# Where the preparation steps of a later block are written in a loop over sixteen experts: from the ninth expert on, five each, instead of from the second on, two each

## The chip, the cores and the metric

The kernel runs on one core of a Trainium2 chip. The metric is the device time of one execution in microseconds (us), as a median of several runs. One more execution was profiled; its span goes from the first to the last instruction.

The core has five engines that run side by side, each with its own queue of instructions in a fixed order: TensorE (PE; its weight loads stand as PEld), VectorE (DVE), ScalarE (ACT), GpSimd (POOL) and SyncE (SP), which here only sends off loads. They wait for each other by semaphores. Transfers between HBM and the on-chip memory run on 16 DMA engines.

## The reference, cut to what matters

The reference runs two blocks of two layers each, one after the other, on 256 tokens of width 1024. The second layer of the first block ends in a routed mixture of 16 experts ("the second experts" of this kernel). The second block begins with a layer that has a state-space part (S5).

```python
def expert_block(args):                      # routed_moe, for each expert
    xblk, e = args
    hid = jax.nn.silu(xblk @ w_gate[e]) * (xblk @ w_up[e])
    return hid @ w_down[e]
...
def s5_ssm(u, a_re, a_im, log_dt, b_re, b_im, c_re, c_im, d_skip, glu_w, glu_b):
    lam = lax.complex(a_re, a_im)
    dt = jnp.exp(log_dt)[:, None]
    lam_bar = jnp.exp(lam * dt)
    b_bar = ((lam_bar - 1.0) / lam)[..., None] * b_mat
    bu = jnp.einsum('bsgh,gph->bsgp', ug, b_bar)
    _, states = lax.associative_scan(combine, (a_seq, bu), axis=1)
    y = jnp.real(jnp.einsum('bsgp,ghp->bsgh', states, c_mat))
```

The scan of the state-space part needs things that depend on its weights alone: dt, the powers of lam_bar, b_bar and a layout of C. They don't need the experts' results, so the kernel computes them beside the experts.

## The kernel before, in words

The second experts are `run_small`. For each expert e of 0 to 15 it needs 12 MB of weights, in twelve loads of 1 MB (`wload`, L172): four for gate, four for up, four for down. All loads go through SP's queue, in the order up(e), gate(e+1), down(e), up(e+1). Their buffers are a ring of 14 (`NW`, pool `W`); other stages and tables take buffers of the same ring. The ring is full when the loop starts.

Per expert TensorE computes the gate product G and the up product U (L1303, 32 matmuls each), four transposes of the hidden rows (L1348, into the PSUM buffer "tp", of which there is one here), and the down product Y (L1303, 32 matmuls). Beside them it gathers the rows of the expert after next (`rows`, xp L1475 and rs L1481; xp uses "tp" as well) and adds the finished expert to its token rows (acc, L1507). ScalarE applies silu to G (L1317). VectorE multiplies by U (s, L1328), copies the transposed hidden rows (hTe, L1349), scales the gathered rows (L1485 to L1487) and weights Y (L1498). As written, the order within an expert is: rows(e+1), up(e), the acc of e-1, **the side steps**, gate(e+1) with the hidden transposes of e in its middle, down(e).

The side steps are those of the generator `ssm_prep`, called by `side_step` (L1558). `side_step` ties the instructions of a step behind the current expert's s on VectorE, and behind an earlier instruction on GpSimd; on the other engines nothing ties them. The Tile scheduler lays down the final order of each engine, and hands out the buffers of a pool.

`ssm_prep` yields 22 times, so it has 22 steps with work:

- Step 1 sends loads of a_re, a_im and log_dt from GpSimd, turns them by three transposes through "tp" (L1929) and computes dt on VectorE by a polynomial. Step 2 computes sines, cosines and the exponential on VectorE (L1853 to L1942), step 3 the factors of b_bar (L1948 to L1963).
- Step 4 loads b_re and b_im, forms b_bar (L1980 to L1982) and transposes it in two groups of four through "tp" (L1986), copied to LB by ScalarE.
- Step 5 loads c_re and c_im (L1994), spreads them on VectorE (L1996), and transposes them in two groups through "tp" (L1999). The load buffers are three of a tag, "wl", so that c_im has to wait for the one that step 4 uses to the end.
- Step 6 claims four buffers of the ring of 14 for the rotation tables rotE (`unit`, whose first write of 0.5 KB goes through SP's queue, L153), clears their starts on GpSimd, and doubles the tables' filled length for the first time. Steps 7 to 10 double it again, from 2 to 32 columns; from 32 columns on, each of the four tables has a step of its own (steps 11 to 22). A doubling of one table is four instructions of VectorE (L2025, L2027, L2028, L2030) and two of GpSimd (L2026, L2029).

Before, steps are called two at a time in experts 1 to 14, so that the last one runs at expert 11. The rest of the calls find nothing left.

Of the kernel before, what the change touches and what calls it, by code (L numbers as in the profile page):

```python
# [22 lines left out]
NE = 16  # L23
# [63 lines left out]
class Kern:  # L87
# [1375 lines left out]
    def run_small(self, NT, wg, wu, wd, R, add_ps, over, after, side=None):  # L1463


        nc, w, ps, CB = self.nc, self.wk, self.ps, 64
        ld = lambda W: (lambda k: self.pre.pop(0) if self.pre else self.wload(W, k, 2, 0, D))
        acc = [[ps.tile([P, 512], F32, name="acc", tag="acc", bufs=2 * NT) for _ in range(2)] for _ in range(NT)]

        def rows(e):  # L1470
            tp = ps.tile([P, 8, CB], F32, name="xp", tag="tp", bufs=self.tpb)
            for k in range(8):
                for i in range(3):
                    for t in range(NT):
                        nc.tensor.matmul(tp[:, k, :], self.hb[:, t, i, k * P:(k + 1) * P], R["oh"][:, t, e],  # L1475
                                         start=(i == 0 and t == 0), stop=(i == 2 and t == NT - 1))
            xT = w.tile([P, 8, CB], F32, name="xT", tag="xT", bufs=2)
            rs = ps.tile([P, CB], F32, name="rs", tag="G", bufs=1)
            for i in range(3):
                for t in range(NT):  # L1480
                    nc.tensor.matmul(rs, self.rb3[:, t, i], R["oh"][:, t, e], start=(i == 0 and t == 0), stop=(i == 2 and t == NT - 1))  # L1481
            rc = w.tile([P, CB], F32, name="rc", tag="rc", bufs=1)
            nc.scalar.copy(rc, rs)
            gain, shift = (v[:, :, None].to_broadcast([P, 8, CB]) for v in self.gs2)
            nc.vector.tensor_tensor(xT, tp, rc[:, None, :].to_broadcast([P, 8, CB]), op=OP.mult)  # L1485
            nc.vector.tensor_tensor(xT, xT, gain, op=OP.mult)
            self.last_v = nc.vector.tensor_tensor(xT, xT, shift, op=OP.add).ins  # L1487
            return xT

        def sums(e, Y):  # L1490
            ohT = w.tile([P, NT, P], F32R, name="ohT", tag="ohT", bufs=1)
            for t in range(NT):
                nc.vector.tensor_scalar(ohT[:, t], self.K["iota"], tokt[:, t, e:e + 1], None, op0=OP.is_equal)
            yh = w.tile([P, 512], F32R, name="yh", tag="yh", bufs=1)
            yl = w.tile([P, 512], F32R, name="yl", tag="yl", bufs=1)
            wr = R["wrow"][:, e:e + 1]
            yt = w.tile([P, 512], F32, name="yt", tag="yt", bufs=1)
            nc.vector.scalar_tensor_tensor(yt, Y, wr, self.g2, op0=OP.mult, op1=OP.mult)  # L1498
            nc.scalar.copy(yh, yt)
            nc.vector.tensor_tensor(yl, yt, yh.bitcast(F32), op=OP.subtract)  # L1500

            def f():
                for c in range(2):
                    for t in range(NT):
                        r = slice(64 * c, 64 * c + 64)
                        for y in (yh, yl):
                            nc.tensor.matmul(acc[t][c], ohT[r, t], y[r], start=(e == 0 and y is yh), stop=(e == NE - 1 and y is yl))  # L1507
            return f

        def ahead(k):  # L1510

            if k < 2:
                return ld(wd[0])(k)
            v = [self.hl.tile([P, 1024], F32, name="wa", tag=tag) for tag in ("wh", "wl")]
            for i in range(2):
                nc.sync.dma_start(v[i], wd[0][(k + i) * P:(k + i + 1) * P, :])
            return v

        xT = rows(0)
        first = self.last_v  # L1520
        s = self.gate(CB, xT, ld(wg[0]))
        with self.tc.issue_after(first):
            R.pop("rest")()
        tokt = w.tile([P, NT, NE], F32, name="tokt", tag="tokt", bufs=1)
        for t in range(NT):
            nc.vector.tensor_scalar(tokt[:, t], R["tokf"], -float(P * t), None, op0=OP.add)
        pend = None
        for e in range(NE):
            if side and e == NE - 1:
                while self.side_step(side):  # L1530
                    pass
            xn = rows(e + 1) if e + 1 < NE else None
            self.up(CB, s, xT, ld(wu[e]))
            if e == NE // 2:
                self.late = [self.last_v, self.last_s, self.last_m, self.last_dma]
            if pend:
                pend()
            for _ in range(2):
                if side and 0 < e < NE - 1:
                    self.side_step(side)  # L1540
            hT = []
            old = s
            turn = lambda: hT.append(self.hidden_T(CB, old))
            if e + 1 < NE:
                s = self.gate(CB, xn, ld(wg[e + 1]), turn)
            else:
                turn()
            xT = xn
            pend = sums(e, self.down(CB, None, ld(wd[e]) if e else ahead, None, None, hT[0]))
        self.gains2()  # L1550
        pend()
        for c in range(2):
            for t in range(NT):
                add_ps(t, c, acc[t][c], c)
        over()
        after()
# [887 lines left out]
```

## Time and profile before

| | us |
|---|---|
| median of 3 runs | 2193.2 (2193.14 to 2193.75) |
| profiled execution, its time | 2193.03 |
| profiled execution, its span | 2191.5 |
| PE busy in the span | 1984.8 (91%) |
| VectorE busy | 1397.7 (64%) |
| ScalarE busy | 954.7 (44%) |
| GpSimd busy | 305.3 (14%) |

Busy shares are means over stages that differ. The second experts run from 1,284 us (first gate product) to 1,758 us (last sum), so what bears on the change is read from this stretch.

### The profile page before, as it was taken

To read this page: it belongs to the slowest core of one execution; us is meant where nothing else is said; L and a number is where in the kernel's file an instruction comes from. 1 tells how busy PE (TensorE), PEld (TensorE's weight loads), DVE (VectorE), ACT (ScalarE), POOL (GpSimd) and SP (SyncE) were. 2 spreads that over 40 slices of the span, in tenths; PEclk is the share of its full clock that TensorE was granted. 3 is DMA by queue.
4 is the path that set the end of the run, shared out by engine and by line. 5 is a ranking of instruction groups with operands and counts; after the bars stand their busy time and mean duration, and the time that the engine had idled before them with its cause. 6 is when DMAs were issued, how large, how long until landed. Compare 5 with 4: busy or idle time off the path is not lost. (4 is left out here: it accounts for less than half of the span.)

```text
span 2191.5 us, 30093 instructions
## 1 busy us (share of the span) xinstructions
PE 1984.8 (91%) x11482; PEld 1357.3 (62%) x11483; DVE 1397.7 (64%) x2526; ACT 954.7 (44%) x1435; POOL 305.3 (14%) x370
## 2 busy tenths in 40 slices
PE   6999979969999999998979979899888889898998
PEld 2877654647778888776675533333333266776997
DVE  3457666669999999888757644332331179576767
ACT  2435315437778787776545610000000032555443
POOL 1201122140000000011020010110100025231111
PEclk9999989979999999999999989999999999989999
DMA  8544367749999999999332579999999954425460
GB/s 251 135 145 136 135 239 273 289 164 351 366 369 389 379 389 388 378 348 332 140 117 58 214 304 353 389 408 409 408 409 409 406 172 143 137 97 181 158 209 20
DMA packets 191307, 580.52 MB, mean 265 GB/s; under 512 B 18736, under 2 KB 49904, under 8 KB 186032
## 3 DMA queue, kind: packets, MB, share of 16 engines
q1 hardware_dynamic: 176656, 550.03, 67.7%
q0 software_dynamic: 7760, 23.26, 3.6%
q10 hardware_dynamic: 6736, 5.21, 0.8%
q8 instruction: 93, 1.52, 0.3%
q14 instruction: 62, 0.51, 0.1%
HBM read 568.41 MB, written 10.03 MB: 264 GB/s over the span
## 5 line engine op out<-in xcount | busy, mean ns | idle before, releaser
L189 DVE TENSOR_TENSOR wl<-wch,wh 128x1024 fp32r<-128x1024 f32 x518 | 631.5, 1239 | 146.3 <-ACT wh L188 129.7
L188 ACT CAST wh<-wch 128x1024 fp32r<-128x1024 f32 x524 | 545.6, 1053 | 292.0 <-PE pj L210 63.6
L211 PE MATMUL pj<-h,wl 128*128 128x256 f32 x448 | 131.0, 293 | 6.3 <-DVE wl L189 6.3
L209 PE MATMUL pj<-h,wh 128*128 128x256 f32 x448 | 130.9, 294 | 3.3 <-ACT h L487 1.3
L210 PE MATMUL pj<-h,wh 128*128 128x256 f32 x448 | 130.4, 292 | 0.0
L1317 ACT ACTIVATE s<-G 128x512 f32<-128x512 f32 x16 | 9.6, 597 | 274.1 <-PE G L1303 274.1
L1303 PE MATMUL G<-wch,xT 128*64 128x512 f32 x512 | 126.5, 621 | 1.2 <-DMA wch<-in_moe_w_gate_dram 1.2
L1303 PE MATMUL U<-wch,xT 128*64 128x512 f32 x512 | 119.8, 599 | 3.7 <-DMA wch<-in_moe_w_up_dram 3.2
L1303 PE MATMUL Y<-wch,hTe 128*64 128x512 f32 x488 | 110.5, 597 | 6.8 <-DMA wch<-in_moe_w_down_dram 5.3
L210 PE MATMUL G<-wl,xu 128*128 128x512 f32 x256 | 103.0, 402 | 5.0 <-DVE wl L189 4.8
L210 PE MATMUL U<-wl,xu 128*128 128x512 f32 x256 | 102.8, 402 | 3.3 <-DVE wl L189 2.3
L209 PE MATMUL U<-wh,xu 128*128 128x512 f32 x256 | 101.5, 397 | 3.2 <-ACT wh L188 3.2
L210 PE MATMUL Y<-wl,hu 128*128 128x512 f32 x256 | 102.8, 402 | 1.4 <-DVE wl L189 1.2
L209 PE MATMUL Y<-wh,hu 128*128 128x512 f32 x256 | 100.7, 393 | 2.6 <-ACT wh L188 2.4
L209 PE MATMUL G<-wh,xu 128*128 128x512 f32 x256 | 101.3, 396 | 0.0
L211 PE MATMUL U<-wh,xu 128*128 128x512 f32 x256 | 100.5, 393 | 0.0
L211 PE MATMUL Y<-wh,hu 128*128 128x512 f32 x256 | 100.5, 393 | 0.0
L211 PE MATMUL G<-wh,xu 128*128 128x512 f32 x256 | 100.1, 391 | 0.0
L211 PEld LDWEIGHTS pj<-h,wl 128*128 128x128 f32 x448 | 88.4, 198 | 9.6 <-DVE wl L189 7.1
L209 PEld LDWEIGHTS pj<-h,wh 128*128 128x128 f32 x448 | 88.5, 198 | 6.9 <-ACT wh L188 2.5
L210 PEld LDWEIGHTS pj<-h,wh 128*128 128x128 f32 x448 | 88.7, 198 | 1.9 <-issue 1.7
L209 PE MATMUL mm<-wh,hTh 128*128 128x256 f32 (+1 forms) x256 | 81.1, 318 | 3.5 <-DVE Y L693 1.8
(667 smaller groups left out, 4185.3 us busy)
## 6 DMA issues: line engine op xcount, KB each, us to landing
wch<-in_moe_w_gate_dram SPq DMA_DIRECT2D x128, 1024.0 KB, 8.0
wch<-in_moe_w_up_dram SPq DMA_DIRECT2D x128, 1024.0 KB, 9.0
wch<-in_moe_w_down_dram SPq DMA_DIRECT2D x125, 1024.0 KB, 8.3
wch<-in_ada_w_dram SPq DMA_DIRECT2D x40, 1024.0 KB, 6.6
wch<-in_even_w_in_dram SPq DMA_DIRECT2D x34, 1024.0 KB, 5.6
wch<-in_odd_w_in_dram SPq DMA_DIRECT2D x16, 1024.0 KB, 5.5
wch<-in_even_w_out_dram SPq DMA_DIRECT2D x10, 1024.0 KB, 5.0
wch<-in_ada_w_dram SPq DMA_DIRECT2D x32, 256.0 KB, 6.6
```

Of the source, the lines that this page charges most:

```text
L188: self.last_h = nc.scalar.copy(h, v).ins
L189: self.last_l = e.tensor_tensor(l, v, h.bitcast(F32), op=OP.subtract).ins
L209: m(out, lh, rh, start=first, stop=False, skip_group_check=chk)
L210: m(out, lh, rl, start=False, stop=False, skip_group_check=chk)
L211: self.last_m = m(out, ll, rh, start=False, stop=last, skip_group_check=chk).ins
L1303: self.last_m = nc.tensor.matmul(out[f * 64:f * 64 + 64, :], x[:, k, :], v[k - k0][:, f * 512:(f + 1) * 512], start=(k == 0), stop=(k == 7 ...
L1317: self.last_s = nc.scalar.activation(s, G, AF.Silu).ins
```

## The change

The loop that calls the side steps calls five instead of two, and from expert 8 (the ninth) instead of expert 1. The 22 steps so fall on experts 8, 9, 10, 11 (five each) and 12 (two). Nothing that is computed changes.

```diff
@@ -1535,8 +1535,10 @@
             if pend:
                 pend()
-            for _ in range(2):
-                if side and 0 < e < NE - 1:
+
+
+            for _ in range(5):
+                if side and NE // 2 <= e < NE - 1:
                     self.side_step(side)
             hT = []
             old = s
```

## Rows read from the trace of the kernel before

**Rows 1.** The page, part 2: GB/s moved, in 40 equal slices.
```profile
GB/s 251 135 145 136 135 239 273 289 164 351 366 369 389 379 389 388 378 348 332 140 117 58 214 304 353 389 408 409 408 409 409 406 172 143 137 97 181 158 209 20
```

**Rows 2.** Stretches from U to U: length, busy us by engine, PEclk, DMA, GB/s.
```profile
1343.70:1377.10 33.40, 29.68 (x174) 10.80 (x172) 11.99 (x36) 2.60 (x5) 1.66 (x10) 0.95 0.91 344
...
1467.45:1495.20 27.75, 26.01 (x166) 9.55 (x164) 7.32 (x17) 1.43 (x3) 1.99 (x4) 1.00 1.02 408
...
1583.10:1615.20 32.10, 27.61 (x166) 10.18 (x164) 11.79 (x17) 1.43 (x3) 2.87 (x2) 0.95 1.02 408
...
1674.60:1705.30 30.70, 26.75 (x164) 9.02 (x164) 5.37 (x10) 1.43 (x3) 0.00 (x0) 1.00 1.02 409
```

**Rows 3.** The same view, in stretches of 30 us.
```profile
1350.00:1380.00 30.00, 26.22 (x157) 9.70 (x155) 11.51 (x34) 2.60 (x5) 1.66 (x10) 0.94 0.90 336
...
1380.00:1410.00 30.00, 26.64 (x165) 10.02 (x163) 7.38 (x27) 2.49 (x5) 2.20 (x13) 0.94 1.00 380
```

**Rows 4.** SP's timeline: start, us, line, operation, output<-input, count.
```profile
1342.23 7.15 SPq L172 DMA_DIRECT2D wch<-in_moe_w_up_dram  x4
...
1351.31 13.11 SPq L153 DMA_DIRECT2D rotE<-in_const_dram  x4
...
1366.55 7.67 SPq L172 DMA_DIRECT2D wch<-in_moe_w_gate_dram  x4
```

**Rows 5.** PE's timeline, expert 2; in brackets idle time before, its releaser.
```profile
1352.82 1.89 PE L1303 MATMUL G<-wch,xT 128*64 128x512 f32 x8
...
1358.34 0.89 PE L1986 MATMUL tp<-c_ident,pr 128*128 128x128 f32 x4 [3.64 <-DVE pr L1982]
...
1359.17 3.31 PE L1303 MATMUL G<-wch,xT 128*64 128x512 f32 x6
...
1364.00 0.66 PE L1348 MATMUL tp<-c_ident,s 128*128 128x128 f32 x4
```

**Rows 6.** PE's timeline, experts 6, 10 and 13.
```profile
1477.54 0.66 PE L1348 MATMUL tp<-c_ident,s 128*128 128x128 f32 x4 [0.79 <-DVE s L1328]
...
1488.26 7.09 PE L1303 MATMUL Y<-wch,hTe 128*64 128x512 f32 x32
...
1600.29 1.60 PE L1475 MATMUL xp<-ohb,hb 128*128 128x64 bf16 x36 [2.86 <-DVE hTe L1349]
...
1674.57 1.94 PE L1303 MATMUL U<-wch,xT 128*64 128x512 f32 x8 [0.61 <-DMA wch<-in_moe_w_up_dram]
```

**Rows 7.** Stretches of side steps on VectorE (columns as in rows 2).
```profile
1326.41:1339.92 13.51, 13.51 (x115) 5.55 (x113) 12.73 (x82) 0.81 (x2) 0.00 (x0) 1.00 1.03 409
...
1353.64:1360.76 7.12, 3.48 (x14) 1.19 (x11) 6.70 (x28) 0.59 (x1) 0.00 (x0) 0.85 1.03 408
...
1419.24:1423.14 3.90, 2.56 (x14) 1.03 (x15) 3.90 (x34) 0.00 (x0) 2.84 (x14) 1.00 1.03 412
...
1448.06:1453.44 5.38, 4.24 (x20) 1.57 (x21) 5.28 (x32) 0.00 (x0) 3.60 (x13) 1.00 1.02 404
...
1505.13:1507.60 2.47, 2.33 (x12) 0.90 (x12) 2.47 (x9) 0.00 (x0) 1.23 (x2) 1.00 1.04 415
...
1562.74:1567.11 4.37, 2.52 (x12) 1.00 (x13) 4.37 (x9) 0.00 (x0) 2.33 (x2) 1.00 1.02 409
...
1593.06:1599.56 6.50, 4.24 (x20) 1.57 (x21) 6.50 (x9) 0.00 (x0) 2.87 (x2) 1.00 1.02 409
...
1625.14:1629.95 4.81, 4.24 (x20) 1.57 (x21) 4.81 (x9) 0.00 (x0) 0.00 (x0) 1.00 1.02 409
```

**Rows 8.** POOL's second C load; landing times of both C loads.
```profile
1361.05 0.75 POOL L1994 DMA_DIRECT2D pr<-in_ssm_c_im_dram  x1 [42.92 <-DVE pr L1982]
...
DMA to landing us min/median/max: 5.1/6.7/8.2
```

**Rows 9.** VectorE's timeline: a hidden copy, a product s.
```profile
1364.70 0.69 DVE L1349 COPY hTe<-tp 128x512 f32<-128x512 f32 x1 [3.94 <-PE tp L1348]
...
1476.80 0.69 DVE L1328 TENSOR_TENSOR s<-s,U 128x512 f32<-128x512 f32 x1 [3.11 <-PE U L1303]
```

## The prediction

> **What bounds the kernel now.** I read the page's 40 slices first [rows 1]: in slices 27 to 32 (1,424 to 1,753 us) the second experts load at 406 to 409 GB/s and nothing else in the kernel stays at that rate so long, so the change lies in a stretch near its load limit. Next, the stretches from one expert's up product U to the next one's [rows 2]. Numbered from 0, expert 6 takes 27.75 us, expert 10 takes 32.10 and expert 13 takes 30.70. Expert 13 is paced by loads: its U begins when its load lands, at 1,674.57 [rows 6]. Twelve loads of 1 MB in 30.7 us are 2.56 us a load. Expert 6 never waits for a load: 27.7 us is TensorE's own pace, so **TensorE has 3.0 us of slack per expert**. It starts with a full ring of 14 loaded buffers and has used this lead up only by expert 13, because the side steps stop it on the way.
>
> Loads therefore set the end: the last experts wait for them, and a load lost anywhere is lost for good. Where are they lost? In 30 us windows [rows 3]: 336 GB/s at 1,350 to 1,380 and 380 at 1,380 to 1,410, against 409 when full [rows 2]. (73 + 29) GB/s x 30 us are 3.06 MB, or **7.5 us at 409 GB/s**. The load queue shows why [rows 4]: after the up loads at 1,342 the four rotE writes hold it from 1,351.31 to 1,364.42, because each waits for a weight buffer to come free, and the next gate load goes out at 1,366.55. So early, most of the ring of 14 holds data that TensorE has not reached, and few loads are under way to bridge such a pause.
>
> **What the change does, part by part.** The 22 steps that do work (five of preparation, 17 of the rotation tables) run at experts 8 to 12 (5, 5, 5, 5, 2) instead of 1 to 11 (2 each). No instruction is added or removed.
>
> **1. The ring of weight buffers.** The rotE buffers are claimed after the up loads of expert 9, not of expert 3. TensorE's pace brings it to U of expert 8 at 1,343.7 + 6 x 27.7 = 1,509.9 [rows 2]. The loads allow it at 1,674.57 - 5 x 30.7 - 7.5 = 1,513.6 [rows 2, 3, 6]. So TensorE will by then wait for loads, nearly all free buffers are queued loads (up to 12, or 31 us), and four small writes no longer drain that queue. The pause of rows 4 goes: **-7.5 us** (between 0, if as much is lost at the new place, and -7.5).
>
> **2. The first batch, at expert 8.** Each preparation step that transposes takes the one PSUM buffer "tp". So do the transposes of the hidden rows (L1348) that the down product needs. Rows 5 show that they get it in the order written: at expert 2 the product s was ready, yet L1348 ran at 1,364.00, behind the transposes of L1986 (first at 1,358.34, for which TensorE had stood 3.64 us). With five steps ahead of it, L1348 of expert 8 queues behind the whole preparation. Its length: steps 1 and 2 take 13.5 us on VectorE [rows 7], of which some 2.7 are four copies and products of the experts at 0.69 [rows 9]; steps 3 and 4 take 7.1; together 17.9. Then the second C load goes out only when step 4 has released its buffer (POOL stood until L1982, 1,361.05) and lands 5.1 to 8.2 us later, median 6.7 [rows 8]. Until now an expert's work lay between; in one batch VectorE waits for it, with the hidden copy queued behind. The product s, the C product, transposes, copies and hand-overs are about seven pieces of 0.6 to 0.7 us [rows 5, 9], 4.5. Sum: 17.9 + 6.7 + 4.5 = 29.1 us from s to the down product (27.5 to 30.6). Without side steps that way is 1,488.26 - 1,476.80, or 11.5 us (L1348 follows s by 0.74) [rows 6, 9]. The down product is **17.6 us late** (16 to 19). What hides some of it is only the gate product of 7 us, and that is in the 11.5. After the idle time the clock is down: six matmuls took 3.31 us after the 3.64 us stop, where eight take 1.89 at full clock [rows 5], so +1.9. Together 19.5 (16 to 22). The loads a_re to the first C load don't move: POOL has no other work here and sends them as soon as their buffers are free.
>
> **3. The later batches, experts 9 to 12.** The hidden copy stands behind the table steps on VectorE. Before, two such steps took from 2 to 6.5 us [rows 7], where six of nine such stretches stand, and TensorE waited 2.86 us for the copy at the longest [rows 6]: 6.5 less 3.65 that 16 gate matmuls cover. With all 32 the cover is 7.3 (1.85 for each eight more [rows 5]). Now: expert 9 some 2 (the first, smallest tables; not shown, taken as half of the next) + 3.9 + 5.4 = 11.3, less 7.3, plus 1.9 of low clock: 5.9. Expert 10: 2 x 2.47 + half of 4.37 = 7.1, less 3.65: 3.5. Expert 11: 1.5 x 4.37 + 6.5 = 13.1, less 7.3, plus 1.9: 7.7. Expert 12: 4.81 - 3.65 = 1.2. **Sum 18** (8 if the copy slips in between steps that wait for POOL; 25 if the cover stays at 16 matmuls).
>
> Two equal batches in rows 7 took 6.50 us with POOL busy for 2.87 us beside them and 4.81 with POOL idle, so POOL's share of a table step slows VectorE's. The Trainium skill (GPSIMD Engine Reference, section 1, Specifications) says that GpSimd's SBUF interfaces are shared with VectorE and contend with VectorE instructions of two SBUF inputs. That agrees with the two rows, and it speaks against packing five such steps together.
>
> **The sum.** From U of expert 8 to U of expert 15 there are seven stretches with 3.0 us slack, 21 us, plus 2.0 for one gather of rows fewer (expert 15 is the last) and 0.8 because the last down product need not wait for loads: 23.8. Late at the end: 19.5 + 18 - 23.8 = 13.7 us behind loads that themselves come 7.5 us earlier: **+6.2 us**. Everything after the experts begins when they end, so it moves along. The profiled execution took 2,193.03 us (span 2,191.5), 0.17 below the median of the runs: 2193.03 + 6.2 = 2,199.2, and on the median some **2,199 us**.
>
> **The rivals.**
> (a) Faster: the hidden transposes don't queue behind the preparation, or VectorE's batches fall into TensorE's waits for loads. For it: at expert 8 TensorE waits for loads anyway, and in rows 5 gate matmuls run between the side transposes. Against it: L1348 in rows 5. Then lateness stays under the 23.8 us of slack, loads set the end, and the 7.5 us are won: 2,185.7. It decides if parts 2 and 3 together cost less than 24 us rather than 37.5.
> (b) No change: the gain is eaten up just so, 31.3 us of stops: 2,193, if the C load lands in 5.1 us and the later batches cost some 13.
> (c) Much slower: POOL beside VectorE stretches all batches as in rows 7 (1.35 times), and 24 + 22 us of stops end 22 us behind the loads: 2193.2 - 7.5 + 22.2 = 2,208.
> (d) It does nothing: the scheduler keeps the order of the engines. Against it: steps are tied behind the current expert's product s. 2,193.
>
> **How the numbers follow.** Chances: the forecast, with ends from 2,195 to 2,204, 0.50; (a) 0.22; (b) 0.15; (c) 0.10; (d) 0.03. A measurement of this kernel tells 0.2% (4.4 us) from no change. Of the forecast's half some 0.12 lies below 2,197.6; of (b) all is within. Faster 0.23 (all of (a) and a rest), same 0.32, slower 0.45. The range takes in (a)'s time and most of (c): 2,186 to 2,207; its ends are the full gain with no lateness, and stops of 45 us in all.
>
> **What would show it.** The pause of rows 4 at 1,350 to 1,410 should be gone (409 GB/s there); TensorE should wait for loads by expert 7; a stop of 12 to 19 us should stand at expert 8, ended by L1999 or L1348; the last experts should run at 27.7 us without waiting for loads. If they wait for loads to the end, (a) is right. A load gap at the new place of the rotE writes would refute part 1.

## The result and the profile after

The changed kernel takes 2,207.1 us as a median of four runs (2,205.8 to 2,210.7), against 2,193.5 for the kernel before beside it (2,193.1 to 2,195.7). The ratio is 1.0054, with a 95% interval of 1.0037 to 1.0071. It is **slower**, by 8 to 16 us (0.4 to 0.7%). The forecast was slower by some 6 (2,199); the median lies 0.1 us beyond the upper end of the range. So the sign was right, and the size was rather less than half of what came (13.6).

The profiled execution took 2,210.65 us (span 2,209.1), 17.6 more than that of before. As the stage begins at slightly different times in the profiled executions, its length is counted below from the first gate product to the start of the last sum: 1,284.5 to 1,758.1 before, **473.5 us**, and 1,286.8 to 1,776.4 after, **489.5 us**. The stage thus holds 16.0 of the 17.6 us. (The profiled execution of the changed kernel is the longest of its four, 3.5 us above their median, so the stage shows somewhat more than the medians do.) This length is given for every experiment as "the stage".

First, stretches of 30 us of the kernel after, in the columns of [rows 2]:

```profile
1350.00:1380.00 30.00, 28.37 (x175) 10.31 (x176) 5.87 (x11) 1.43 (x3) 0.00 (x0) 1.00 1.03 409
1380.00:1410.00 30.00, 27.58 (x172) 9.94 (x169) 6.07 (x10) 1.43 (x3) 0.00 (x0) 1.00 1.02 409
1650.00:1680.00 30.00, 19.63 (x126) 7.24 (x122) 15.13 (x18) 1.43 (x3) 7.93 (x6) 0.83 0.76 291
```

The first two answer [rows 3]: where 336 and 380 GB/s stood there are 409 now. In the third, loads have fallen to 291 GB/s, and TensorE is busy for 19.6 us of 30: there the loads fall behind because TensorE stands and frees no buffers. Next, the stretches from U to U of experts 8 to 12:

```profile
1515.50:1566.20 50.70, 34.23 (x181) 13.06 (x181) 21.59 (x111) 4.84 (x9) 2.00 (x12) 0.80 0.95 367
1566.20:1601.00 34.80, 27.71 (x164) 10.71 (x164) 17.15 (x92) 0.87 (x3) 10.43 (x43) 0.85 0.87 331
1601.00:1635.40 34.40, 28.88 (x166) 10.88 (x164) 12.83 (x29) 1.43 (x3) 5.92 (x10) 0.90 0.95 368
1635.40:1674.70 39.30, 28.14 (x166) 10.18 (x164) 20.88 (x29) 1.43 (x3) 10.39 (x8) 0.87 0.83 327
1674.70:1703.50 28.80, 25.99 (x166) 9.55 (x164) 10.11 (x17) 1.43 (x3) 0.00 (x0) 1.00 1.01 400
```

Experts 2 to 5 of this kernel take 27.55 us each (from U of expert 2 at 1,344.6 to U of expert 6 at 1,454.8), so that the five stretches are 23.2, 7.3, 6.9, 11.8 and 1.3 us too long, some **50** in all. POOL, for whose work beside the experts only a rival of the prediction had a price of its own, is busy for 10.4 us in the second and the fourth.

How expert 8 is stopped is seen on TensorE, in the columns of [rows 5]:

```profile
1541.59 1.09 PE L1988 MATMUL tp<-c_ident,pr 128*128 128x128 f32 x4 [5.21 <-DVE pr L1984]
1544.15 1.09 PE L1988 MATMUL tp<-c_ident,pr 128*128 128x128 f32 x4 [1.47 <-DVE pr L1984]
1545.91 1.11 PE L2001 MATMUL tp<-c_ident,pr 128*128 128x128 f32 x4 [0.68 <-ACT LB L1989]
1551.17 1.09 PE L2001 MATMUL tp<-c_ident,pr 128*128 128x128 f32 x4 [4.15 <-DVE pr L1998]
1552.95 1.11 PE L1348 MATMUL tp<-c_ident,s 128*128 128x128 f32 x4 [0.69 <-ACT LCb L2006]
1554.85 9.91 PE L1303 MATMUL Y<-wch,hTe 128*64 128x512 f32 x32 [0.78 <-DVE hTe L1349]
```

The product s came at 1,525.15, on VectorE:

```profile
1525.15 0.69 DVE L1328 TENSOR_TENSOR s<-s,U 128x512 f32<-128x512 f32 x1 [3.79 <-PE U L1303]
```

The down product Y starts at 1,554.85, 29.7 us later. L1348 stands behind all four groups of preparation transposes (L1988 and L2001, which are L1986 and L1999 of before, two lines further down). Y then takes 9.91 us instead of 7.09 [rows 6]; the granted clock is 0.50, the lower of its two levels, from 1,545 to 1,560.

And how experts 9 to 12 are stopped:

```profile
1574.92 3.65 PE L1303 MATMUL G<-wch,xT 128*64 128x512 f32 x16
1585.37 0.32 PE L1475 MATMUL xp<-ohb,hb 128*128 128x64 bf16 x3 [6.79 <-DVE hTe L1349]
1585.62 3.68 PE L1303 MATMUL G<-wch,xT 128*64 128x512 f32 x8
...
1611.72 3.65 PE L1303 MATMUL G<-wch,xT 128*64 128x512 f32 x16
1619.27 2.08 PE L1475 MATMUL xp<-ohb,hb 128*128 128x64 bf16 x36 [3.90 <-DVE hTe L1349]
...
1646.06 5.37 PE L1303 MATMUL G<-wch,xT 128*64 128x512 f32 x24
1661.66 1.12 PE L1475 MATMUL xp<-ohb,hb 128*128 128x64 bf16 x18 [10.23 <-DVE hTe L1349]
...
1690.17 1.21 PE L1475 MATMUL xp<-ohb,hb 128*128 128x64 bf16 x36 [1.18 <-DVE hTe L1349]
```

Each time the gathering product xp, which writes "tp", waits for VectorE to empty it by the hidden copy hTe: 6.79, 3.90, 10.23 and 1.18 us. Ahead of xp stand 16, 16 and 24 gate matmuls at experts 9, 10 and 11. Eight gate matmuls right behind the first stop take 3.68 us; at full clock eight take 1.89 [rows 5].

### The profile page after: what moved, and what is told of

Its sections match the earlier page's. It is cut to its first block, busy times and chain, and to the rows that moved or that the text cites. A ratio compares the mean times of both kernels' runs of the same rounds, so it can differ in the third digit from the quotient of the medians.

```text
span 2209.1 us, 30098 instructions
## 1 busy us (share of the span) xinstructions
PE 1991.6 (90%) x11482; PEld 1365.9 (62%) x11483; DVE 1402.9 (64%) x2526; ACT 955.1 (43%) x1435; POOL 306.3 (14%) x370
## 3 DMA queue, kind: packets, MB, share of 16 engines
q10 hardware_dynamic: 6736, 5.21, 0.8%
q8 instruction: 93, 1.52, 0.3%
```

## The experiments

All ratios are to the kernel before on the same chip, with 95% intervals. Unless it is said otherwise, a diff is against the changed kernel.

**1. The second C load.** A buffer of another tag lets the load go out early, so that VectorE doesn't wait for it.

```diff
-                tc_ = hl("pr3", "wl")
+                tc_ = hl("pr3", ("wl", "wh")[c])
```

> The changed kernel with one edit: the buffer of the second C load comes from another tag, so that the load goes out with the first ones at about 1,318 us instead of behind step 4 of expert 8. Theory A (TensorE's stops at experts 8 to 12 set the end): VectorE's wait of 6.3 us for that load at expert 8 goes, the down product of expert 8 starts some 6 us earlier, and the whole is 5 to 7 us shorter than the changed kernel, about 2,201 us. Theory B (the loads that are missing after the new place of the four rotE writes set the end): that place and the ring are as before, so the time stays at 2,207.

Measured: 1.0071 (1.0048 to 1.0095), the stage 486.7 us. Theory A missed: the stage is 2.8 us shorter, and the runs show no gain (the changed kernel had 1.0054). B's time came; whether B's cause is at work, experiment 2 tells. VectorE's wait for the load is gone, but TensorE's timeline shows what was behind it:

```profile
1540.26 1.08 PE L1988 MATMUL tp<-c_ident,pr 128*128 128x128 f32 x4 [5.77 <-DVE pr L1984]
...
1544.58 1.12 PE L2001 MATMUL tp<-c_ident,pr 128*128 128x128 f32 x4 [0.68 <-ACT LB L1989]
1546.88 1.12 PE L2001 MATMUL tp<-c_ident,pr 128*128 128x128 f32 x4 [1.18 <-ACT LCa L2004]
...
1550.58 1.98 PE L1303 MATMUL Y<-wch,hTe 128*64 128x512 f32 x4 [0.78 <-DVE hTe L1349]
```

Here s came some 27.3 us ahead of Y, against 29.7: the four groups of transposes still go one by one through the one buffer "tp", and the third, the fourth and L1348 each wait for ScalarE to empty it. In the changed kernel VectorE had waited 6.34 us for the load; 2.4 us of this were on the path.

**2. All calls behind the hidden transposes.** The loop is the same, written behind the gate product's call, which has the hidden transposes inside.

```diff
-            for _ in range(5):
-                if side and NE // 2 <= e < NE - 1:
-                    self.side_step(side)
...
                 turn()
+            for _ in range(5 if NE // 2 <= e < NE - 1 else 0):
+                if side:
+                    self.side_step(side)
             xT = xn
```

> The changed kernel with the calls of the side steps moved within the expert, behind the gate product and the hidden transposes and ahead of the down product; same experts, five each. Theory A: neither the hidden transposes nor the hidden copy stand behind side steps any more. At expert 8 the preparation (29 us) runs beside the down and up products, and only the rows of expert 10 wait for it, some 2 us; the stops of 7, 4 and 10 us at experts 9 to 11 go. Loads set the end, without the early gap: 7.5 us below the kernel before, about 2,186. Theory B: the rotE buffers are claimed at the same point within four loads, so most of the loss stays, about 2,205.

Measured: 0.9975 (0.9964 to 0.9986), the stage 467.7 us. A is right in kind: with the order of TensorE's and VectorE's queues turned round, the same steps at the same experts are faster than both kernels, though expert 8 costs more than A had it (experiment 3). What TensorE waited for in the waits view, of this kernel from 1,500 to 1,700 us:

```profile
PE tp L1987 <- DVE pr L1983: 5.6, 1, 5.6
PE rs L1481 <- ACT s L1317: 4.9, 7, 0.7
```

No wait of xp for hTe is left (22.1 us in the kernel after), and the loads stay at 404 to 409 GB/s from 1,350 to 1,740 us. B falls: the four rotE writes go out at 1,550.15 here, and the stretch behind them is full:

```profile
1560.00:1590.00 30.00, 28.52 (x204) 11.08 (x200) 18.59 (x94) 1.81 (x4) 10.97 (x52) 1.00 1.03 404
```

From 1,672 on TensorE waits for loads.

**3 and 4. Half of it each.** Either expert 8's batch or those of experts 9 to 12 go behind the hidden transposes.

```diff
-            for _ in range(5):
-                if side and NE // 2 <= e < NE - 1:
+            for _ in range(5 if NE // 2 < e < NE - 1 else 0):
+                if side:
...
                 turn()
+            for _ in range(5 if e == NE // 2 else 0):
+                if side:
+                    self.side_step(side)
```

> As the changed kernel, but the five calls of expert 8 stand behind the calls of gate(e+1) and the hidden transposes; the calls of experts 9 to 12 stay where the change puts them. Takes away the stop at expert 8 alone. By the theory (the two stops add up against 24 us of slack): the 22 us of stops and some 7 us of low clock at experts 9 to 12 stay, some 7 us of stops of transposes behind the preparation come at expert 8, so some 36 of stops against 23.8 of slack, loads 7.5 us earlier: 2193.5 + 12 - 7.5, about 2198 (2194 to 2201). Rival (the stop at expert 8 is the whole loss, the later copies are covered): about 2188, as with all calls behind the hidden transposes.

Measured: 1.0039 (1.0023 to 1.0055), the stage 483.0 us. The rival falls; the theory is right in kind, and its number came some 4 us too low. The reason stands in TensorE's timeline of this kernel:

```profile
1540.80 1.08 PE L1990 MATMUL tp<-c_ident,pr 128*128 128x128 f32 x4 [5.63 <-DVE pr L1986]
1541.81 3.67 PE L1303 MATMUL Y<-wch,hTe 128*64 128x512 f32 x6
```

Behind the hidden transposes, the preparation's transposes stand in the middle of the down product instead, stop it for 5.63 us and slow it. U to U of expert 8 is 43.5 us: 16 us too long, not 7. So that place saves only some 7 of the 23 us at expert 8, and the kernel of experiment 2 bears the other 16, too (43.5).

With the halves exchanged (expert 8 stays, experts 9 to 12 move):

```diff
-            for _ in range(5):
-                if side and NE // 2 <= e < NE - 1:
+            for _ in range(5 if e == NE // 2 else 0):
+                if side:
...
                 turn()
+            for _ in range(5 if NE // 2 < e < NE - 1 else 0):
+                if side:
+                    self.side_step(side)
```

> The other half: expert 8's five calls stay ahead of the gate call as in the changed kernel, those of experts 9 to 12 stand behind the hidden transposes. By the theory: the stop at expert 8 is 18 us longer than without side steps plus 2.8 of low clock, 21 in all, under the 23.8 us of slack, the stops for the hidden copy go: loads set the end again, 2186 to 2189. Rival (the loads that stood still while TensorE stood at expert 8 are lost for good): 2198 or more.

Measured: 0.9993 (0.9976 to 1.0009), the stage 470.6 us. That lies between the two. The stop at expert 8 alone does fit into the slack, as TensorE waits for loads again at the end (from 1,703 us), but not for nothing. Loads fall behind in one stretch (same columns):

```profile
1560.00:1590.00 30.00, 29.76 (x224) 11.68 (x222) 14.73 (x85) 1.43 (x3) 9.19 (x48) 0.98 0.96 363
```

The 46 GB/s missing for 30 us are 3.4 us at 409 GB/s, about the 2.9 us by which the stage is longer than in experiment 2. The load queue shows where they come from: the four rotE writes hold it for 12.67 us while TensorE stands at expert 8 (Y starts at 1,556.20), against 6.61 in experiment 2.

```profile
1549.87 12.67 SPq L153 DMA_DIRECT2D rotE<-in_const_dram  x4
```

Taken from the change, the later batches bring 18.9 us of the stage, the first one 6.5.

**5. GpSimd's products on VectorE.** The forecast had mis-sized the later batches, and POOL was busy in just those. So its two products per table doubling go to VectorE, which then has six instructions instead of four.

```diff
-                nc.gpsimd.tensor_tensor(tt[0], ei, S, op=OP.mult)
+                V.tensor_tensor(tt[0], ei, S, op=OP.mult)
...
-                nc.gpsimd.tensor_tensor(tt[1], ei, C, op=OP.mult)
+                V.tensor_tensor(tt[1], ei, C, op=OP.mult)
```

> The changed kernel, with the two GpSimd products of every table doubling on VectorE instead. In the changed kernel VectorE's products of 128x256 take 1.27 us while GpSimd works beside them and 0.42 else, those of 128x512 1.52 and 0.68; the batch of expert 11 takes 15.6 us from s to the hidden copy. Theory (GpSimd beside it stretches VectorE): all products take 0.42 and 0.68, so that the batch of expert 11 needs 18 at 0.335 us and 12 at 0.605, 13.3 us, although it has ten instructions more, and TensorE's stop there falls from 10.2 to about 8 us; the batch of expert 12 grows by 2.4, as GpSimd had done its share ahead; the time changes little: 2204 to 2208. Rival (the stretch comes from something else, as the loads): the long products stay long and the batch of expert 11 grows to 18 us or more; 2210 or more.

Measured: 0.998 (0.9966 to 0.9993), the stage 473.2 us. The theory is right on the instructions and wrong on the time, in the good direction. VectorE of the kernel after first, in expert 11's batch:

```profile
1646.68 0.42 DVE L2027 TENSOR_TENSOR rotE<-rotE,pr 128x256 f32<-128x256 f32 x1
1647.01 1.27 DVE L2030 TENSOR_TENSOR rotE<-rotE,sct 128x256 f32<-128x256 f32 x1
...
1652.74 0.68 DVE L2027 TENSOR_TENSOR rotE<-rotE,pr 128x512 f32<-128x512 f32 x1
1653.35 1.52 DVE L2030 TENSOR_TENSOR rotE<-rotE,sct 128x512 f32<-128x512 f32 x1
...
1660.93 0.68 DVE L1349 COPY hTe<-tp 128x512 f32<-128x512 f32 x1
```

GpSimd beside it:

```profile
1646.84 1.15 POOL L2028 TENSOR_TENSOR pr<-rotE,sct 128x512 f32<-128x512 f32 x1 [26.96 <-DVE rotE L2032]
...
1652.90 1.42 POOL L2028 TENSOR_TENSOR pr<-rotE,sct 128x512 f32<-128x512 f32 x1 [0.70 <-DVE rotE L2032]
```

The product at 1,647.01 takes 1.27 us where its like takes 0.42; it ends at 1,648.28, 0.29 us behind the end of GpSimd's (1,647.99). The one at 1,653.35 takes 1.52 instead of 0.68 and ends 0.55 behind GpSimd's. VectorE of this kernel:

```profile
1637.59 0.41 DVE L2030 TENSOR_TENSOR rotE<-rotE,sct 128x256 f32<-128x256 f32 x1
...
1644.56 0.68 DVE L2032 TENSOR_TENSOR rotE<-rotE,pr 128x512 f32<-128x512 f32 x1
...
1647.57 0.68 DVE L1349 COPY hTe<-tp 128x512 f32<-128x512 f32 x1
```

All take 0.42 and 0.68, and the way from s to the hidden copy is 13.3 us (1,634.30 to 1,647.57) where it was 16.2 (1,644.73 to 1,660.93), with nine instructions more (a tenth stands behind the copy). That is 2.9 us. The rest of the gain is in TensorE's order:

```profile
1574.98 7.09 PE L1303 MATMUL G<-wch,xT 128*64 128x512 f32 x32
1586.30 1.32 PE L1475 MATMUL xp<-ohb,hb 128*128 128x64 bf16 x36 [4.23 <-DVE hTe L1349]
...
1607.46 5.37 PE L1303 MATMUL G<-wch,xT 128*64 128x512 f32 x24
1614.00 1.21 PE L1475 MATMUL xp<-ohb,hb 128*128 128x64 bf16 x36 [1.17 <-DVE hTe L1349]
...
1635.63 7.09 PE L1303 MATMUL G<-wch,xT 128*64 128x512 f32 x32
...
1648.30 0.32 PE L1475 MATMUL xp<-ohb,hb 128*128 128x64 bf16 x3 [4.55 <-DVE hTe L1349]
```

The scheduler now laid xp behind 32, 24 and 32 gate matmuls instead of 16, 16 and 24, and the stops are 4.23, 1.17 and 4.55 us. Why it did so the traces don't show, and no run tested it. Of the 11.0 us by which these three stops fell (20.9 to 10.0), the cover of 16, 8 and 8 more matmuls explains 6.9 (1.72 for eight). The batches explain 3.1: from s to the copy they take 12.2, 7.1 and 13.3 us instead of 11.3, 8.1 and 16.2, so that of expert 9 grew. The last 1.0 is rs (L1481, 0.34 us behind a wait of 0.69), which at expert 11 now runs ahead of xp. U to U of experts 9 to 12 is 10.9 us too long in all (30.5, 28.2, 34.1 and 28.3), where it was 27.1: that is the gain of the stage against the changed kernel.

Against the kernel before, the profiled execution shows no gain (a stage of 473.2 us against 473.5). It is 2.6 us above the median of its ten runs (2,192.9 against 2,190.3); what the runs win against the kernel before is not located.

**6 and 7. The same on two other kernels:** on that of experiment 2 (6), and on the kernel before (7); the diff is against these.

```diff
-                nc.gpsimd.tensor_tensor(tt[0], ei, S, op=OP.mult)
+                V.tensor_tensor(tt[0], ei, S, op=OP.mult)
...
-                nc.gpsimd.tensor_tensor(tt[1], ei, C, op=OP.mult)
+                V.tensor_tensor(tt[1], ei, C, op=OP.mult)
```

> Both cures at once: the calls of five per expert from expert 8 behind the hidden transposes, and no GpSimd products. If loads set the end with either cure alone (the loads run at 404 to 409 GB/s throughout), the two together give no more than one: 2187 to 2190. If stops of TensorE still cost with either, it is faster than both: 2184 to 2186.

Measured: 0.997 (0.9958 to 0.9982), the stage 466.2 us. It is the lowest median of all (2,185.6) and lies where the second theory put it, but the interval overlaps that of experiment 2 (and experiment 10 has as low a ratio), so these runs don't tell whether two cures give more than one. Loads set the end here and in experiment 2, where TensorE waits for them from 1,666 and 1,672 us on. In experiment 5 they don't: there TensorE waits for no load behind 1,534 us, and its own pace sets the end.

> The kernel before, with the two GpSimd products of every table doubling on VectorE. If GpSimd beside VectorE is a cost of the kernel before as well: its stops for the hidden copy (2.9 us at the longest) go, but the pause of the load queue at 1,350 to 1,410 stays, and loads set the end: 2191 to 2194, near no change. If those stops are what brings the last experts to their loads late: 2188 to 2190.

Measured: 1.0002 (0.9987 to 1.0017), the stage 473.8 us. Waits of xp for hTe fall from 11.6 to 3.3 us, and nothing is won: loads still run at 337 and 379 GB/s in the stretches of [rows 3], and loads set the end.

**8 and 9. Is it the claim of the rotE buffers, or TensorE's stop, that makes the load queue pause early?** First the preparation is early and the claim late, in the old place.

```diff
-            for _ in range(5):
-                if side and NE // 2 <= e < NE - 1:
+            for _ in range(5 if NE // 2 <= e < NE - 1 else {1: 2, 2: 2, 3: 1}.get(e, 0)):
+                if side:
```

> The five preparation steps at experts 1 to 3 as in the kernel before (2, 2, 1), the 17 table steps five per expert from expert 8 on. Theory A: the stop of 17 us and the low clock after it at expert 8 go; the table batches, now at experts 8 to 11, keep their 22 us of stops and some 7 us of low clock. 29 less 23.8 us of slack leave 5 us, against 7.5 won by the late claim: 2 to 3 us below the kernel before, about 2,191. Theory B: 2,207, since the claim stands one expert earlier and the table batches follow it as now.

Measured: 1.0001 (0.9985 to 1.0017), the stage 473.2 us. Theory B falls, and A's 2,191 lies within the interval. What it tells of the claim is in the stretches of 30 us:

```profile
1350.00:1380.00 30.00, 26.36 (x159) 9.92 (x157) 10.88 (x35) 1.98 (x4) 0.75 (x1) 0.94 1.02 404
1380.00:1410.00 30.00, 28.17 (x174) 10.46 (x172) 6.54 (x12) 3.11 (x6) 0.00 (x0) 1.00 1.02 409
1590.00:1620.00 30.00, 18.84 (x92) 6.43 (x88) 18.39 (x26) 0.62 (x1) 10.40 (x8) 0.83 0.90 359
```

TensorE stops at expert 2 as before (3.6 us for the same transposes), yet loads run at 404 and 409 GB/s. So the stop alone makes no pause. What was won is lost again in the table batches at experts 8 to 11, where TensorE waits 22.4 us for hTe in all.

The opposite is the kernel before (two steps per expert from expert 1) with its calls behind the hidden transposes, as in experiment 2. Against the kernel before:

```diff
-            for _ in range(2):
-                if side and 0 < e < NE - 1:
-                    self.side_step(side)
...
                 turn()
+            for _ in range(2 if 0 < e < NE - 1 else 0):
+                if side:
+                    self.side_step(side)
```

> As the kernel before (two steps per expert from expert 1), with the calls behind the gate call and the hidden transposes. The rotE buffers are still claimed early, at expert 3. If the early claim itself costs the loads (the step of the prediction): the pause of the load queue stays, and only TensorE's stops go, which loads cover at the end: 2191 to 2194. If the pause came only from TensorE's stop at expert 2 (no buffer came free while it stood): it goes with the stop, and the time is 2186 to 2188, as with the late place behind the hidden transposes.

Measured: 0.9991 (0.998 to 1.0002), the stage 472.8 us, near no change. The pause stays, only one expert later, as the claim does, and TensorE is busy for 28.4 of the 30 us:

```profile
1380.00:1410.00 30.00, 28.38 (x201) 10.99 (x199) 8.44 (x28) 3.11 (x6) 2.60 (x20) 1.00 0.83 314
```

SyncE's timeline of this kernel, around the claim:

```profile
1361.57 7.12 SPq L172 DMA_DIRECT2D wch<-in_moe_w_gate_dram  x4
1374.99 10.88 SPq L153 DMA_DIRECT2D rotE<-in_const_dram  x4
```

So **the early claim alone makes the pause**.

**10 and 11. A claim neither early nor in one lump.** One step per expert at experts 1 to 5, two from expert 6 on, so that the claim comes at expert 6; once behind the hidden transposes (10), once in the old place (11), where it takes the place of the loop of five.

```diff
+            for _ in range((2 if e > 5 else 1) if 0 < e < NE - 1 else 0):
+                if side:
+                    self.side_step(side)
```

> One step per expert at experts 1 to 5, two from expert 6 to 14, all calls behind the gate call and the hidden transposes. The rotE buffers are claimed at expert 6, and no expert has more than two steps. By the theory (loads set the end, all that helps is to keep them going and to stop TensorE less than its slack): 2185 to 2187, the least of all. If the early claim of the four buffers does not matter: the same as two steps per expert from expert 1 at the same place, whatever that gives.

Measured: 0.9966 (0.9952 to 0.998), the stage 468.2 us.

> One step per expert at experts 1 to 5, two from expert 6 on, called at the place of the kernel before (ahead of the gate call). Against the kernel before: the claim of the four rotE buffers moves from expert 3 to expert 6, and the preparation is spread over five experts. If the early claim is what costs the loads, the pause of the load queue at 1,350 to 1,380 goes, loads stay at 404 to 409 GB/s, and the time is 2187 to 2190 although the steps still stand ahead of the hidden transposes. If the place ahead of the hidden transposes is what costs: 2192 to 2194.

Measured: 0.9974 (0.9961 to 0.9986), the stage 468.6 us. Against experiment 9, which differs from experiment 10 only in the rates, the stage is 4.6 us shorter, and the loads of experiment 10 run at 405 to 409 GB/s from 1,350 us on. The rates also spread the preparation; since loads set the end of both kernels, the later claim is the likelier cause. The place matters little when no expert has more than two steps.

**12. Five per expert, but from expert 1.**

```diff
-            for _ in range(5):
-                if side and NE // 2 <= e < NE - 1:
+            for _ in range(5 if 0 < e < NE - 1 else 0):
+                if side:
```

> Five steps per expert, but from expert 1 on (done at expert 5). Theory A: the same stops of some 50 us in all, now while the ring is full of data that TensorE hasn't reached, so that loads stand still while TensorE does, and the slack of the later experts can only be used as far as loads come: 15 to 25 us above the kernel before, 2,208 to 2,218. If it were the late place and not the batches that cost time, it would be at or below the kernel before, 2,185 to 2,194.

Measured: 1.0133 (1.0106 to 1.016), the stage 502.1 us: the theory is right in kind, and the loss is larger than it said. Much the same stops (20.1 us for hTe and 10.5 for the preparation; in the changed kernel 22.1 and 10.8) cost 12.6 us more than at experts 8 to 12. The stretches of 30 us from 1,320 show 213 and 278 GB/s; from expert 10 on loads pace TensorE at some 31 us per expert, and nothing of the loss is caught up. The late place as such was no mistake.

## Why the prediction was right or wrong

**What bounds it, and step 1 (the ring): right, somewhat too large.** The pause went, 409 GB/s stand in its place, and TensorE waited for a load first at U of expert 7 (1,483.2 us), as forecast. Experiments 8 and 9 show that the claim makes the pause. At its new place the four writes hold the queue for 7.10 us (from 1,537.46), and the loads still move 395 GB/s and more up to 1,550. The price of the pause was set at 7.5 us; the stage without later losses is 5.8 us shorter than before (experiment 2), and experiments 9 and 10 give 4.6. What makes up the difference is open.

**Step 2 (expert 8): the right size, with one wrong cause in it.** From s to Y it was 29.7 us, forecast 29.1, behind L1348 as forecast; between rs and Y TensorE has only the five groups of transposes for 18.5 us, the longest single wait being 5.21. But the term of 6.7 us for the second C load (VectorE waited 6.34) lay mostly beside other work: experiment 1 took it away and saved 2.4. Beside it runs the chain of the four groups through one buffer, with ScalarE's copies and the hand-overs, of which the prediction took too little into its 4.5 us. The low clock cost 2.8 us on Y, not 1.9, and xp (1.6 us) came behind Y. In all U to U was 23.2 us too long, forecast 19.5.

**Step 3 (the later batches): the step that failed.** Forecast 18, measured 27.1 (7.3, 6.9, 11.8, 1.3). Two of the batches were sized well: from the end of s to hTe they take 10.6 and 7.5 us at experts 9 and 10, forecast 11.3 and 7.1. What was wrong is the cover: 32 matmuls (7.3 us) were assumed at experts 9 and 11, where the changed kernel has 16 and 24, 3.65 and 5.37 us: 5.6 us of cover that wasn't there. The bound of 25 us "if the cover stays at 16 matmuls" was the right reading; it was not taken. At expert 11 GpSimd beside VectorE comes on top: four products of 128x256 and four of 128x512, each about 0.85 us longer, 6.8 us of the 15.6 from the first of them to the copy (20 instructions alone would be 8.8). The forecast had scaled rows in which some of this was already contained [rows 7], and got 13.1, some 2.4 too little. And the stops of experts 9, 10 and 11 each bring a stretch of low clock, where two of 1.9 us were counted.

Beside [rows 7], the prediction named a rule of the Trainium skill (GPSIMD Engine Reference, section 1, Specifications) that speaks against packing these steps. Experiment 5 bears it out for the instructions, 1.27 against 0.42 us; a large part of the gain came by the order that the scheduler chose.

**The sum.** From U of expert 8 to U of expert 15, the forecast gives 7 x 27.7 - 2.0 + 37.5 = 229.4 us; the trace shows 240.0 (1,515.5 to 1,755.5). The 10.6 are +3.7 of step 2, +9.1 of step 3, less 2.2 for a pace of 27.55 and a shorter last stretch. They stand against the 9.8 us between the stage's +16.0 and the forecast's +6.2. That TensorE, and not loads, sets the end was right: behind 1,533.4 us it waits for no load. Stops of 50.2 us in all are 5 more than the 45 at the upper end of the range; that the median still lies at that end is in part luck, as the pace and the last stretch gave back 2.2 us, and as the median is 3.5 us below the profiled execution.

**The rivals.** (c) has nearly the time that came (2,208), by stops of 46 us; 50.2 came. Its mechanism, GpSimd beside VectorE, is real, but the larger part of its price is cover, as experiment 5 shows. (a) is wrong for this kernel; experiment 2 shows that it is right for the same steps behind the hidden transposes. (b) and (d) fall with the stops.

## What to carry to other kernels

Before side work is packed into fewer, larger batches, look at what stands behind it in each engine's queue: the same five steps per expert cost 16 us of the stage ahead of the hidden transposes, and won 6 behind them. Cover is a count of instructions that the scheduler lays ahead of the wait; it is read from the trace for the very place, or taken at its lower bound. And a small write that claims buffers of a load ring goes where the consumer already waits for loads, not where the ring is full.

## What the runs showed of the hardware

A VectorE product of two operands, begun while GpSimd runs one, ended 0.29 us (128x256) or 0.55 us (128x512) after GpSimd's, close to the 0.33 and 0.60 us from one such instruction to the next when VectorE is alone: as if it had stood until GpSimd had finished, and had run then. The Trainium skill (SBUF — State Buffer, section "SBUF: two separate sides") says just that: the two engines' shared ports go to one instruction whole, and the other engine blocks until it ends. The rows agree.

So GpSimd gave nothing while it worked beside VectorE: in the long doublings, four VectorE instructions beside two of GpSimd took longer than all six on VectorE (4.10 us from 1,652.74 to 1,656.84 against 3.6 for six at 0.60). What GpSimd had done ahead of a batch did help: the way from s to the hidden copy at expert 12 is 5.4 us with it and 7.2 without.
